# One compression gather's row copies placed behind the FFN, its loads a step ahead, and cached keys first in the sample attention's values

## The chip, the cores and the metric

The kernel runs on one core of one Trainium2 chip. The metric is device time in microseconds (us) of one launch that does the whole step; three runs of the kernel before the change gave 2105.78, 2105.80 and 2107.84, median 2105.8. The core has a matrix engine (PE, TensorE), VectorE (DVE), ScalarE (ACT), GpSimd (POOL) and a queue engine (SP) that issues most DMAs. Each engine works through its own instructions strictly in order and waits on semaphores of the others, so an instruction that waits also holds what is queued behind it on its engine.

## The reference

The model is two layers of a decoder over 576 tokens: 512 of a prompt and 8 each of 8 sample requests with 256 cached tokens. Layer 0 (even) mixes by a convolution and stick-breaking attention, layer 1 (odd) by sparse attention with compressed, selected and window branches. After each mixer come cross attention to a memory and a SwiGLU FFN. All is float32. What the change touches:

```python
def stick_breaking(q, k, v, q_pos, k_pos):     # k, v: cached rows, then the new ones
...
    w = jnp.where(mask, jnp.exp(jax.nn.log_sigmoid(z) + log_after), 0.0)
    return jnp.einsum('bhqk,bkhd->bqhd', w.astype(v.dtype), v)

def compress_blocks(kv, pe, w1, w2):           # odd layer, for k and for v
...
    blk = kv.reshape(B, nb, CMP_BLK, G, d) + pe[None, None, :, None, :]
    hid = jax.nn.gelu(jnp.einsum('bnlgd,ldh->bngh', blk, w1))
    return jnp.einsum('bngh,he->bnge', hid, w2)

def swiglu(a, w_gate, w_up, w_down):
    return (jax.nn.silu(a @ w_gate) * (a @ w_up)) @ w_down
```

The values of the attention are a sum over keys, so the order in which cached and new keys are added is free. The cached rows that the compression reads don't depend on anything computed, so they may be read at any time.

## The kernel before, in words

Activations lie feature by token in SBUF. Each large product takes float32 operands split in a high and a low part and is done as three products (high by high L308, low activation L309, low weight L310) summed in PSUM. Weights are loaded by SP into `raw` (three buffers), split by ACT (`wh`, L259) and DVE or POOL (`wl`, L261, L263) into two buffers each. Accumulators `acc` and transposes `wk` have four PSUM buffers each.

In the FFN, `fast.block` computes gate and up columns (L1172 to L1174, with `ga` and `gb` in PSUM; ACT keeps a sum in `gu`, L1255). DVE multiplies (`sg`, L1361), ACT and DVE make the halves `fH` and `fL` (L1366, L1367). `dense` then multiplies the down weights with these; after each accumulator DVE scales it (L1335) and adds it to the residual `h` (L341), which frees the accumulator.

The FFN of layer 0 goes in three chunks of columns. In the last (`c0 == 16`), a `tick` within the down product pumps a generator, `cmp_gather("k", 0, ...)`: the first quarter of the odd layer's compression, for which it reads the cached rows page by page. A gather has four steps; in each, four DMAs on SP (L1310, 64 KB each, 32 partitions) fill the first half of a buffer `cn` from the pool `knp` (three buffers, shared with others), DVE copies it regrouped into the second half (L1311), PE transposes it (L1316), and ACT and DVE evacuate it into `bt`. Three more gathers (second half of k, both of v) run in the odd layer's input product.

A scheduler lays down each engine's order from the order of the source, with priorities and the waits that it foresees; the generators only say where in the source a piece stands. So the first gather's copies stood on DVE between the last products of the FFN's block.

In the sample attention (two groups of four requests), the weights of the cached keys are transposed and evacuated into `wo` (two tiles, 128x512), those of the new tokens into `wn` (64x512); then `values` sums weights by values for four requests into `so` (L783): new tokens (`sbs`) first, then the cached keys from tiles that `take` loads (`sv`). In the trace these tiles read `vx` as they share a buffer of that name.

Of the kernel before, what the change touches and what calls it, by code (L numbers as in the profile page):

```python
# [94 lines left out]
def hybrid_step(ctx: ExitStack, tc: tile.TileContext, off, a, o):  # L95
    nc = tc.nc
# [17 lines left out]
    def KN(name):  # L114
        return knp.tile([128, 1024], FT, tag="kn", name=name)
# [41 lines left out]
    ident = cp.tile([128, 128], FT, name="ident")  # L157
# [528 lines left out]
    def sample_sb(sa, X, qT, kT, Vn, OHL):  # L686
# [10 lines left out]
        wn = X[:64, 1280:1792]  # L697
# [12 lines left out]
        for g in range(2):  # L710
# [7 lines left out]
            for b4 in range(4):  # L718
# [5 lines left out]
                for n2 in range(2):  # L724
                    p = WK()
# [33 lines left out]
            for b4 in range(4):  # L759
                x = en[:, b4][:, ::-1]  # L760
                nc.vector.tensor_tensor_scan(x, x, x, initial=1.0, op0=OP.mult, op1=OP.bypass)
                x = eo[:, b4][:, ::-1]
# [5 lines left out]
            wo = OHL[2], X[:, 0:512]  # L768
# [16 lines left out]
                                     skip_group_check=True, **kw)  # L785

            for b4 in range(4):
                values(b4, wn, Vn, start=b4 == 0, stop=False)
            for b4 in range(4):
                V = take()  # L790
                for n2 in range(2):
                    values(b4, wo[n2], V[:, n2 * 512:n2 * 512 + 512], start=False, stop=n2 == 1 and b4 == 3)
                yield 1
            os_ = X[:, 512:1024]
            evac(os_, O)
            yield 1
# [504 lines left out]
    cmp_w = 161  # L1301
    early_rows = {}

    def cmp_gather(x, h16, bt):
        for q4 in range(4):
            kn = KN("cn")
            for i in range(4):
                src = a["cache_nsa_cmp_" + x][0, ds(pages[q4 * 4 + i], 1)] \
                    .rearrange("a (n c l) g d -> (a n) c (l g d)", n=2, l=2)
                nc.sync.dma_start(kn[i * 32:i * 32 + 32, 0:512], src[:, h16 * 16:h16 * 16 + 16])  # L1310
            nc.vector.tensor_copy(kn[:, 512:1024].rearrange("p (g l d) -> p g l d", g=4, l=2),  # L1311
                                  kn[:, 0:512].rearrange("p (l g d) -> p g l d", l=2, g=4))
            yield 1
            p = WK()
            for g in range(4):
                nc.tensor.transpose(p[:, g * 128:g * 128 + 128], kn[:, 512 + g * 128:640 + g * 128], ident)  # L1316
            pv = p.rearrange("p (g b c) -> p g b c", g=4, c=16)
            for g in range(4):
                evac(bt[:, :, q4 * 32:q4 * 32 + 32].rearrange("p c (b g) -> p g b c", g=4)[:, g], pv[:, g])
            yield 1  # L1320


    def cmp_tile():
        return xtp.tile([128, 16 * cmp_w], FT, tag="bt", name="bt").rearrange("p (c n) -> p c n", n=cmp_w)
# [1 line left out]
    def ffn(l, fast, nxt):  # L1326
        wd = a["w_ffn_down"][l]
        kept = []

        def add_f(m, s0, n, p):  # L1330
            for c0, r in rs.items():
                x0, x1 = max(s0, c0), min(s0 + n, c0 + FH)
                if x1 > x0:
                    x = p[:, x0 - s0:x1 - s0]
                    nc.vector.tensor_mul(x, x, r[:, x0 - c0:x1 - c0])  # L1335
            add_h(m, s0, n, p)

        def into(b):
            if not kept:
                kept.extend(BIG(x, FR)[:, 0:4096].rearrange("p (b k m) -> p b k m", b=2, k=8) for x in ("dH", "dL"))  # L1340
            return [x[:, b] for x in kept]

        for c0, nch in ((0, 8), (8, 8), (16, 6)):
            HH, HL = v8(BIG("fH", FR)), v8(BIG("fL", FR))

            def down():
                ready.append(wblock(wd, c0, nch, 0, 256))
                yield 1

            for b0 in range(0, nch, 2):  # L1350
                sg = {}

                def out_gate(m, s0, p, own=False, sg=sg):
                    t = p if own else TMP("sg")[:, :FH]
                    ev_r(t, p, s0)
                    sg[m, s0] = t
                    return lambda: nc.scalar.activation(t, t, AF.Silu)

                def out_up(m, s0, p, own=False, sg=sg, b0=b0):
                    t = sg[m, s0]  # L1360
                    (nc.gpsimd if own else nc.vector).tensor_mul(t, p, t)  # L1361
                    e = nc.vector if b0 + 2 == nch and s0 == (1 - m) * FH else nc.gpsimd

                    def rest():
                        x = HH[:, b0 + m, s0:s0 + FH]
                        nc.scalar.activation(x, t, AF.Copy)  # L1366
                        e.tensor_sub(HL[:, b0 + m, s0:s0 + FH], t, x)  # L1367

                    return rest

                fast.block(out_gate, [])
                if b0 + 2 == nch:
                    later, fast.blocks = fast.blocks, []
                    fast.block(out_up, [down()])
                    fast.blocks = later
                    if not ready:
                        pump([down()], 1)
                else:
                    fast.block(out_up, [])
            if c0 < 16 or l == 0:  # L1380
                n_, rows0 = [0], []
                if c0 == 16:
                    early_rows["k"] = cmp_tile()
                    rows0 = [cmp_gather("k", 0, early_rows["k"])]

                def tick():
                    n_[0] += 1
                    if n_[0] % 5 == 4:
                        pump(rows0, 1)
                    if c0 < 16 and n_[0] == 50:  # L1390
                        fast.take()
                    if c0 < 16 and n_[0] in (54, 56, 58, 60):
                        pump(fast.G[1], 1)

                dense(wd, (HH, HL), c0, nch, 0, 1024, add_f, nxt=nxt if c0 == 16 else None, tick=tick,
                      parts=HV if c0 == 16 else ((0, FH), (FH, FH)))
        if l == 0:
            return
        out = [final(*HV[0])]
        W = [ready.pop(), wblock(wd, c0, nch, 256, 256)]  # L1400
        for s0, n in HV:
            s, late = slice(s0, s0 + n), None
            for m in range(8):
                WH, WL = W[m // 2]
                if s0 == 0 and m in (0, 2):
                    W.append(wblock(wd, c0, nch, m * 128 + 512, 256, into=into(m // 2)))
                ms = slice(m % 2 * 128, m % 2 * 128 + 128)
                p = ACC()[:, :n]
                for k in range(nch):
                    nc.tensor.matmul(p, WH[:, k, ms], HH[:, k, s], start=k == 0, stop=False)  # L1410
                    nc.tensor.matmul(p, WH[:, k, ms], HL[:, k, s], start=False, stop=False)  # L1411
                    nc.tensor.matmul(p, WL[:, k, ms], HH[:, k, s], start=False, stop=k == nch - 1)  # L1412
                    if s0 and k % 2:
                        pump(out, 1)
                if late is not None:
                    add_f(*late)
                late = m, s0, n, p
            add_f(*late)
            if s0 == 0:
                shift_states()  # L1420
        pump(out, 99)
        pump([final(*HV[1])], 99)
# [745 lines left out]
```

## Time and profile before

| | |
|---|---|
| median of three runs | 2105.8 us |
| profiled execution, time | 2100.41 us |
| its span | 2098.5 us |
| mean granted clock of PE | 0.981 |
| PE busy | 1977.1 us, 94% |
| PE weight loads | 86% |
| DVE busy | 1395.6 us, 67% |
| ACT, POOL busy | 46%, 40% |

The times of engines are of the one profiled execution; rows give microseconds from its span's start. PE is the engine that is nearly always busy, so the time is PE's work plus the gaps in it. [...] A row's bracket is the idle time of its engine just before it, with what ended it.

### The profile page before, as it was taken

Reading aid. Unit: us, or ns where it says so; the run is one execution under the profiler, and the core shown is the slowest. Engines: PE = TensorE matmul, PEld = TensorE weight load, DVE = VectorE, ACT = ScalarE, POOL = GpSimd, SP = SyncE. Lnnn points to the kernel's source line nnn. Section 1 sums busy time; section 2 is a strip of 40 time slices with the busy share of each in tenths; the row PEclk is TensorE's granted clock in tenths of the full one; section 3 lists DMA queues with packets and bytes.
Section 4 is the critical chain, followed back from the end, with each engine's and each line's share of the span. In section 5 each row is a group of like instructions: output and inputs, shape, how many; then the busy total and the mean of one; then the engine's idle time right before and its main releaser. Section 6 shows DMA issues by size and latency. Waiting matters only on the chain. (4 is left out here: it accounts for less than half of the span.)

```text
span 2098.5 us, 37416 instructions
## 1 busy us (share of the span) xinstructions
PE 1977.1 (94%) x14641; PEld 1811.3 (86%) x14641; DVE 1395.6 (67%) x2422; ACT 965.6 (46%) x2105; POOL 848.3 (40%) x774
## 2 busy tenths in 40 slices
PE   7999988999999999998899989999899989999998
PEld 6988855987889999998889967778887989999998
DVE  5469887544588577584646777765544787586675
ACT  5344555443455245153324537665444555254352
POOL 4355584422155235153313335563511355154252
PEclk9999998999999999999999999999999999999999
DMA  7445133255323222233344122212356222232323
GB/s 234 150 158 171 61 119 108 79 170 162 123 72 91 91 81 85 87 93 108 101 125 145 46 64 86 84 53 51 125 163 195 66 79 86 85 94 82 95 71 150
DMA packets 200797, 225.11 MB, mean 107 GB/s; under 512 B 13399, under 2 KB 179351, under 8 KB 200549
## 3 DMA queue, kind: packets, MB, share of 16 engines
q1 hardware_dynamic: 198317, 214.34, 32.7%
q0 software_dynamic: 2304, 8.39, 1.3%
q8 instruction: 115, 1.88, 0.4%
q14 instruction: 61, 0.50, 0.1%
HBM read 210.04 MB, written 17.08 MB: 108 GB/s over the span
## 5 line engine op out<-in xcount | busy, mean ns | idle before, releaser
L308 PE MATMUL acc<-aH,wh 128*128 128x256 f32 (+2 forms) x912 | 283.1, 310 | 2.5 <-DVE hpb L467 2.5
L263 POOL TENSOR_TENSOR wl<-raw,wh 128x1024 fp32r<-128x1024 f32 (+1 forms) x68 | 159.4, 2348 | 285.1 <-ACT wh L259 264.6
L310 PE MATMUL acc<-aH,wl 128*128 128x256 f32 (+2 forms) x912 | 272.6, 299 | 0.0
L309 PE MATMUL acc<-aL,wh 128*128 128x256 f32 (+2 forms) x912 | 271.7, 298 | 0.0
L259 ACT ACTIVATE wh<-raw 128x1024 fp32r<-128x1024 f32 (+1 forms) x174 | 167.3, 992 | 210.6 <-PE acc L309 77.2
L308 PE MATMUL acc<-fH,wh 128*128 128x288 f32 (+2 forms) x608 | 180.7, 297 | 3.1 <-DVE h L341 3.1
L309 PE MATMUL acc<-fL,wh 128*128 128x288 f32 (+2 forms) x608 | 180.6, 297 | 3.1 <-DVE fL L1367 3.1
L310 PE MATMUL acc<-fH,wl 128*128 128x288 f32 (+2 forms) x608 | 180.3, 297 | 0.2 <-POOL wl L263 0.2
L308 PEld LDWEIGHTS acc<-aH,wh 128*128 128x128 f32 (+1 forms) x912 | 173.7, 190 | 7.4 <-issue 3.3
L309 PEld LDWEIGHTS acc<-aL,wh 128*128 128x128 f32 (+1 forms) x912 | 173.6, 190 | 3.0 <-issue 2.5
L310 PEld LDWEIGHTS acc<-aH,wl 128*128 128x128 f32 (+1 forms) x912 | 173.0, 190 | 3.2 <-issue 2.9
L261 DVE TENSOR_TENSOR wl<-raw,wh 128x1024 fp32r<-128x1024 f32 (+1 forms) x106 | 144.2, 1373 | 31.3 <-ACT wh L259 27.6
L1139 POOL TENSOR_TENSOR wl<-raw,wl 128x512 fp32r<-128x512 f32 x44 | 69.0, 1569 | 187.2 <-ACT wl L1138 142.9
L1958 POOL TENSOR_TENSOR nar<-nar,f 128x512 f32<-128x512 f32 (+3 forms) x128 | 93.8, 755 | 88.0 <-DVE f L1956 60.6
L309 PEld LDWEIGHTS acc<-fL,wh 128*128 128x128 f32 x608 | 115.1, 189 | 4.2 <-DVE fL L1367 4.2
L308 PEld LDWEIGHTS acc<-fH,wh 128*128 128x128 f32 x608 | 115.0, 189 | 3.6 <-DVE h L341 3.3
L310 PEld LDWEIGHTS acc<-fH,wl 128*128 128x128 f32 x608 | 115.1, 189 | 0.4 <-POOL wl L263 0.4
L1367 POOL TENSOR_TENSOR fL<-sg,fH 128x288 fp32r<-128x288 f32 x76 | 77.7, 1023 | 59.0 <-ACT fH L1366 59.0
L341 DVE TENSOR_TENSOR h<-acc,h 128x288 f32<-128x288 f32 (+2 forms) x176 | 79.5, 454 | 32.1 <-PE acc L310 29.3
L1139 POOL TENSOR_TENSOR wh<-raw,wh 128x512 fp32r<-128x512 f32 x44 | 71.6, 1627 | 62.8 <-ACT wh L1138 62.6
L1335 DVE TENSOR_TENSOR acc<-acc,rs 128x288 f32<-128x288 f32 (+2 forms) x112 | 47.2, 422 | 72.1 <-PE acc L310 66.0
L1172 PE MATMUL gb<-x,wl 128*128 128x288 f32 x264 | 80.3, 304 | 14.1 <-ACT gu L1255 12.2
(540 smaller groups left out, 6402.7 us busy)
## 6 DMA issues: line engine op xcount, KB each, us to landing
raw<-in_w_ffn_gate_dram SPq DMA_DIRECT2D x44, 512.0 KB
raw<-in_w_ffn_up_dram SPq DMA_DIRECT2D x44, 512.0 KB
raw<-in_w_ffn_down_dram SPq DMA_DIRECT2D x40, 512.0 KB
ck<-in_cache_mem_k_dram SPq DMA_DIRECT2D x32, 512.0 KB
cv<-in_cache_mem_v_dram SPq DMA_DIRECT2D x32, 512.0 KB
raw<-in_w_in_even_dram SPq DMA_DIRECT2D x20, 512.0 KB
raw<-in_w_mem_k_dram SPq DMA_DIRECT2D x16, 512.0 KB
raw<-in_w_mem_v_dram SPq DMA_DIRECT2D x16, 512.0 KB
```

Of the source, the lines that this page charges most:

```text
L259: last[1] = nc.scalar.activation(hi, x, AF.Copy)
L261: nc.vector.tensor_sub(lo, x, hi)
L263: nc.gpsimd.tensor_sub(lo, x, hi)
L308: nc.tensor.matmul(po, WH[:, k, ms], H[:, k, s], start=k == 0, stop=False)
L309: nc.tensor.matmul(po, WH[:, k, ms], L[:, k, s], start=False, stop=False)
L310: nc.tensor.matmul(po, WL[:, k, ms], H[:, k, s], start=False, stop=k == nk - 1)
L341: nc.vector.tensor_add(h[:, m, s0:s0 + n], p, h[:, m, s0:s0 + n])
L1139: eng.tensor_sub(L, x, H)
L1172: nc.tensor.matmul(po, WH[:, k], H[:, k], start=start and k == 0, stop=False, skip_group_check=True)
L1335: nc.vector.tensor_mul(x, x, r[:, x0 - c0:x1 - c0])
L1367: e.tensor_sub(HL[:, b0 + m, s0:s0 + FH], t, x)
L1958: nc.gpsimd.tensor_tensor(P[:, x, :n], P[:, x, :n], f[:, x:x + 1].to_broadcast([128, n]), op=OP.mult)
```

## The change

In `values`' callers the cached keys come first and the new tokens last. `cmp_gather` has a new first step that only loads, and loads the next step's rows before it copies the present ones; so it has nine steps instead of eight. For the first gather the copies are tied, in order and not by a semaphore, behind the last DVE instruction that had been issued when the down product of the last chunk begins, and the tick that pumps it comes every fourth time instead of every fifth.

```diff
--- before.py
+++ after.py
@@ -785,12 +785,12 @@
                                      skip_group_check=True, **kw)
 
             for b4 in range(4):
-                values(b4, wn, Vn, start=b4 == 0, stop=False)
-            for b4 in range(4):
                 V = take()
                 for n2 in range(2):
-                    values(b4, wo[n2], V[:, n2 * 512:n2 * 512 + 512], start=False, stop=n2 == 1 and b4 == 3)
-                yield 1
+                    values(b4, wo[n2], V[:, n2 * 512:n2 * 512 + 512], start=b4 == n2 == 0, stop=False)
+                yield 1
+            for b4 in range(4):
+                values(b4, wn, Vn, start=False, stop=b4 == 3)
             os_ = X[:, 512:1024]
             evac(os_, O)
             yield 1
@@ -1301,24 +1301,35 @@
     cmp_w = 161
     early_rows = {}
 
-    def cmp_gather(x, h16, bt):
-        for q4 in range(4):
-            kn = KN("cn")
+    def cmp_gather(x, h16, bt, behind=None):
+        kn = {}
+
+        def load(q4):
+            t = kn[q4] = KN("cn")
             for i in range(4):
                 src = a["cache_nsa_cmp_" + x][0, ds(pages[q4 * 4 + i], 1)] \
                     .rearrange("a (n c l) g d -> (a n) c (l g d)", n=2, l=2)
-                nc.sync.dma_start(kn[i * 32:i * 32 + 32, 0:512], src[:, h16 * 16:h16 * 16 + 16])
-            nc.vector.tensor_copy(kn[:, 512:1024].rearrange("p (g l d) -> p g l d", g=4, l=2),
-                                  kn[:, 0:512].rearrange("p (l g d) -> p g l d", l=2, g=4))
+                nc.sync.dma_start(t[i * 32:i * 32 + 32, 0:512], src[:, h16 * 16:h16 * 16 + 16])
+
+        load(0)
+        yield 1
+        for q4 in range(4):
+            if q4 < 3:
+                load(q4 + 1)
+            t = kn.pop(q4)
+            c = nc.vector.tensor_copy(t[:, 512:1024].rearrange("p (g l d) -> p g l d", g=4, l=2),
+                                      t[:, 0:512].rearrange("p (l g d) -> p g l d", l=2, g=4))
+            if behind is not None:
+                tc.add_manual_dep(c.ins, behind, mybir.DependencyInfo(
+                    mybir.DependencyClass.NoSync, mybir.DependencyReason.DATA), reason="program order")
             yield 1
             p = WK()
             for g in range(4):
-                nc.tensor.transpose(p[:, g * 128:g * 128 + 128], kn[:, 512 + g * 128:640 + g * 128], ident)
+                nc.tensor.transpose(p[:, g * 128:g * 128 + 128], t[:, 512 + g * 128:640 + g * 128], ident)
             pv = p.rearrange("p (g b c) -> p g b c", g=4, c=16)
             for g in range(4):
                 evac(bt[:, :, q4 * 32:q4 * 32 + 32].rearrange("p c (b g) -> p g b c", g=4)[:, g], pv[:, g])
             yield 1
-
 
     def cmp_tile():
         return xtp.tile([128, 16 * cmp_w], FT, tag="bt", name="bt").rearrange("p (c n) -> p c n", n=cmp_w)
@@ -1381,11 +1392,12 @@
                 n_, rows0 = [0], []
                 if c0 == 16:
                     early_rows["k"] = cmp_tile()
-                    rows0 = [cmp_gather("k", 0, early_rows["k"])]
+                    rows0 = [cmp_gather("k", 0, early_rows["k"], next(
+                        i.name for i in reversed(nc.cur_bb.bb.instructions) if str(i.engine).endswith("DVE")))]
 
                 def tick():
                     n_[0] += 1
-                    if n_[0] % 5 == 4:
+                    if n_[0] % 4 == 3:
                         pump(rows0, 1)
                     if c0 < 16 and n_[0] == 50:
                         fast.take()
```

The number of instructions of each engine is the same. Lines below the change move down by 9 to 12 (the copy L1311 is L1320 after, the product L1361 is L1372).

DVE at the end of the last FFN block of layer 0, before (`sg`, `gu`, `fL` belong to the block; `cn` are the gathered rows, `wl` the low halves of down weights):

```order
L1311 COPY cn_10173<-cn_10173 128x512
L242 TENSOR_TENSOR sg_10015<-gb_9848,rs_6409 128x288
L1311 COPY cn_10268<-cn_10268 128x512
L1215 TENSOR_TENSOR acc_9887<-acc_9887,gu_6441 128x288
L242 TENSOR_TENSOR sg_10056<-acc_9887,rs_6415 128x288
L261 TENSOR_TENSOR wl_10031<-raw_10036,wh_10030 128x512
L1311 COPY cn_10356<-cn_10356 128x512
L1361 TENSOR_TENSOR sg_9959<-ga_9980,sg_9959 128x288
L1257 TENSOR_TENSOR sg_10098<-acc_10017,gu_6441 128x288
L1361 TENSOR_TENSOR sg_10015<-gb_9981,sg_10015 128x288
L261 TENSOR_TENSOR wl_10138<-raw_10139,wh_10137 128x1024
L1367 TENSOR_TENSOR fL_9350<-sg_10015,fH_9349 128x288
```

The same stretch after, from the last but one of these rows on (those above it are the same without the three copies):

```order
L261 TENSOR_TENSOR wl_10138<-raw_10139,wh_10137 128x1024
L1378 TENSOR_TENSOR fL_9350<-sg_10015,fH_9349 128x288
L1215 TENSOR_TENSOR acc_10017<-acc_10017,gu_6441 128x288
L1372 TENSOR_TENSOR sg_10056<-acc_10017,sg_10056 128x288
L1526 COPY bt_10136<-vt_93 128x16
L1346 TENSOR_TENSOR acc_10147<-acc_10147,rs_6409 128x256
L1378 TENSOR_TENSOR fL_9350<-sg_10056,fH_9349 128x288
L341 TENSOR_TENSOR h_92<-acc_10147,h_92 128x256
L1320 COPY cn_10166<-cn_10166 128x512
L1320 COPY cn_10199<-cn_10199 128x512
L1320 COPY cn_10282<-cn_10282 128x512
L214 SCALAR_TENSOR_TENSOR aL_10584<-h_92,vt_93,aH_10583 128x256
```

The three copies of cached rows have moved from between the block's products to behind the first sum into `h`.

DVE at the end of the layer's down product, before (`acc` scaled and `h` summed for one output tile after the other, `var` the norm's statistic):

```order
L341 TENSOR_TENSOR h_92<-acc_10514,h_92 128x256
L214 SCALAR_TENSOR_TENSOR aL_10584<-h_92,vt_93,aH_10583 128x256
L1335 TENSOR_TENSOR acc_10535<-acc_10535,rs_6409 128x32
L1335 TENSOR_TENSOR acc_10535<-acc_10535,rs_6415 128x288
L341 TENSOR_TENSOR h_92<-acc_10535,h_92 128x320
L214 SCALAR_TENSOR_TENSOR aL_10584<-h_92,vt_93,aH_10583 128x320
L1335 TENSOR_TENSOR acc_10556<-acc_10556,rs_6409 128x32
L1311 COPY cn_10863<-cn_10863 128x512
L1335 TENSOR_TENSOR acc_10556<-acc_10556,rs_6415 128x288
L261 TENSOR_TENSOR wl_10674<-raw_10675,wh_10673 128x1024
L341 TENSOR_TENSOR h_92<-acc_10556,h_92 128x320
L261 TENSOR_TENSOR wl_10674<-raw_10679,wh_10673 128x1024
```

And after, from the sum of accumulator `acc_10492` on:

```order
L341 TENSOR_TENSOR h_92<-acc_10492,h_92 128x256
L1320 COPY cn_10811<-cn_10811 128x512
L1346 TENSOR_TENSOR acc_10514<-acc_10514,rs_6409 128x256
L214 SCALAR_TENSOR_TENSOR aL_10584<-h_92,vt_93,aH_10583 128x256
L341 TENSOR_TENSOR h_92<-acc_10514,h_92 128x256
L214 SCALAR_TENSOR_TENSOR aL_10584<-h_92,vt_93,aH_10583 128x256
L1346 TENSOR_TENSOR acc_10535<-acc_10535,rs_6409 128x32
L1346 TENSOR_TENSOR acc_10535<-acc_10535,rs_6415 128x288
L341 TENSOR_TENSOR h_92<-acc_10535,h_92 128x320
L214 SCALAR_TENSOR_TENSOR aL_10584<-h_92,vt_93,aH_10583 128x320
L1346 TENSOR_TENSOR acc_10556<-acc_10556,rs_6409 128x32
L1346 TENSOR_TENSOR acc_10556<-acc_10556,rs_6415 128x288
```

The copy that stood between the two scalings of the last tile now stands ahead of three sums into `h`.

PE where the values of the second group begin, before (`sbs` new tokens, `sv` cached keys, `L308` to `L310` the output projection):

```order
L194 MATMUL rsb<-ident,var 128x128 x2
L194 MATMUL rsb<-ident,var 128x64
L783 MATMUL so<-sbs,vx 32x128 x16
L783 MATMUL so<-sv,vx 32x128 x6
L308 MATMUL acc<-oH,wh 128x256
L783 MATMUL so<-sv,vx 32x128 x2
L568 MATMUL wk<-ident,sba 128x128 x2
L783 MATMUL so<-sv,vx 32x128
L309 MATMUL acc<-oL,wh 128x256
L310 MATMUL acc<-oH,wl 128x256
```

And after:

```order
L194 MATMUL rsb<-ident,var 128x128 x2
L194 MATMUL rsb<-ident,var 128x64
L783 MATMUL so<-sv,vx 32x128 x8
L568 MATMUL wk<-ident,sba 128x128
L783 MATMUL so<-sv,vx 32x128 x16
L568 MATMUL wk<-ident,sba 128x128
L783 MATMUL so<-sv,vx 32x128
L568 MATMUL wk<-ident,sba 128x128 x2
L308 MATMUL acc<-oH,wh 128x256
L568 MATMUL wk<-ident,sba 128x128
```

The products on cached keys come first, with transposes of the convolution between them; the 16 on new tokens follow far behind, among the output projection's.

## Rows read from the trace of the kernel before

**Rows 1.** Waits of PE, 930 to 1150 us: who for whom, total, times, longest.

```profile
PE gb L1172 <- ACT gu L1255: 9.7, 1, 9.7
PE hid L1537 <- DMA w<-in_cmp_w_k_dram: 4.6, 3, 2.7
PE rsb L194 <- POOL var L188: 3.7, 1, 3.7
...
PE acc L308 <- DVE h L341: 3.1, 1, 3.1
```

**Rows 2.** Timeline of DVE, 948 to 974 us: start, duration, operation, idle before it.

```profile
953.98 0.75 DVE L1311 COPY cn<-cn 128x512 f32<-128x512 f32 x1 [5.03 <-DMA cn<-in_cache_nsa_cmp_k_dram]
...
961.02 0.43 DVE L1311 COPY cn<-cn 128x512 f32<-128x512 f32 x1 [5.94 <-DMA cn<-in_cache_nsa_cmp_k_dram]
...
962.24 0.68 DVE L261 TENSOR_TENSOR wl<-raw,wh 128x512 fp32r<-128x512 f32 x1
966.68 0.43 DVE L1311 COPY cn<-cn 128x512 f32<-128x512 f32 x1 [3.76 <-DMA cn<-in_cache_nsa_cmp_k_dram]
967.02 0.45 DVE L1361 TENSOR_TENSOR sg<-ga,sg 128x288 f32<-128x288 f32 x1
```

**Rows 3.** Timeline of ACT, 960 to 978 us.

```profile
967.86 0.39 ACT L1255 ACTIVATE gu<-gb 128x288 f32<-128x288 f32 x1
968.15 0.62 ACT L259 ACTIVATE wh<-raw 128x512 fp32r<-128x512 f32 x1
```

**Rows 4.** Timeline of PE, 954 to 976 us.

```profile
968.30 0.61 PE L1172 MATMUL gb<-x,wl 128*128 128x288 f32 x1 [9.67 <-ACT gu L1255]
...
971.29 0.30 PE L1172 MATMUL acc<-x,s4w 128*128 128x288 f32 x1
...
974.33 0.39 PE L309 MATMUL acc<-fL,wh 128*128 128x256 f32 x1
```

**Rows 5.** Timeline of SP's queue, 944 to 975 us.

```profile
945.81 10.08 SPq L1310 DMA_DIRECT2D cn<-in_cache_nsa_cmp_k_dram  x12
962.94 11.36 SPq L271 DMA_DIRECT2D raw<-in_w_ffn_down_dram  x4
```

**Rows 6.** Windows: length, busy by engine (PE, PEld, DVE, ACT, POOL), clock, DMA share, GB/s.

```profile
947.00:955.00 8.00, 8.00 (x61) 7.86 (x60) 2.93 (x5) 2.45 (x5) 2.60 (x3) 1.00 0.12 43
...
1012.00:1019.00 7.00, 5.79 (x22) 5.80 (x23) 6.17 (x14) 2.84 (x8) 2.71 (x3) 0.51 0.56 161
...
1029.00:1034.00 5.00, 5.00 (x27) 5.00 (x27) 1.47 (x5) 1.19 (x3) 0.00 (x0) 0.66 0.31 89
330.00:350.00 20.00, 15.09 (x108) 9.19 (x104) 15.94 (x23) 11.54 (x23) 8.80 (x8) 0.76 0.23 66
```

**Rows 7.** Timeline of DVE, 1004 to 1014 us.

```profile
1009.61 1.41 DVE L1311 COPY cn<-cn 128x512 f32<-128x512 f32 x1 [3.02 <-DMA cn<-in_cache_nsa_cmp_k_dram]
...
1011.53 1.22 DVE L261 TENSOR_TENSOR wl<-raw,wh 128x1024 fp32r<-128x1024 f32 x1
1012.67 0.48 DVE L341 TENSOR_TENSOR h<-acc,h 128x320 f32<-128x320 f32 x1
```

**Rows 8.** Timeline of PE, 1092.5 to 1105 us.

```profile
1093.72 1.36 PE L1537 MATMUL hid<-kvA,w 128*128 128x161 f32 x8 [1.15 <-DMA w<-in_cmp_w_k_dram]
...
1101.07 2.52 PE L1537 MATMUL hid<-kvA,w 128*128 128x161 f32 x8 [2.70 <-DMA w<-in_cmp_w_k_dram]
```

**Rows 9.** Timeline of DVE, 1019 to 1030 us.

```profile
1023.24 0.43 DVE L1311 COPY cn<-cn 128x512 f32<-128x512 f32 x1 [2.84 <-DMA cn<-in_cache_nsa_cmp_k_dram]
...
1027.08 0.15 DVE L187 TENSOR_SCALAR var<-ssp 128x2 f32<-128x2 f32 x1
```

**Rows 10.** Timeline of PE, 336 to 347 us.

```profile
343.83 1.93 PE L783 MATMUL so<-sbs,vx 64*32 64x128 f32 x32 [4.91 <-DVE vx L141]
```

**Rows 11.** Timeline of DVE, 333 to 346 us.

```profile
339.56 0.66 DVE L141 COPY vx<-wk 128x512 f32<-128x512 f32 x1
...
343.10 0.68 DVE L141 COPY vx<-wk 64x512 f32<-64x512 f32 x1
```

## The prediction

> **What bounds the kernel now.** I read the page's busy shares first: PE works 94% of the span, so a gain must come out of PE's idle time or out of stretches at the lower clock, and only two places change. Then PE's waits around the row copies [rows 1]: the list is headed by one wait of 9.7 us of `gb` L1172, and `rsb` 3.7 and `acc` 3.1 belong to the same stage; the reader is to see that each is a single wait. The `hid` waits (4.6 in 3) are for weights loaded through POOL, which the change leaves where they were. The chain behind the 9.7 us follows from DVE's and ACT's timelines. DVE reached its three row copies before their data: it sat 5.03, 5.94 and 3.76 us in front of them [rows 2]. Only behind the third could it do the product `sg` at 967.02, then ACT evacuated `gu` at 967.86 [rows 3], then PE went on at 968.30 [rows 4]. The copies feed nothing that PE needs there; they stand in front of what it needs. The loads can't be faster: 12 loads of 64 KB issued in 10.1 us [rows 5], with a DMA share of 0.12, which is 2 of 16 engines, at 43 GB/s [rows 6]; 256 KB per copy at that pace is 6.1 us, and the copies' ends lie 7.0 and 5.7 us apart [rows 2].
>
> For the other edit the same view of the sample attention shows PE waiting 4.91 us for an evacuation of `vx` before it starts the values [rows 10], and DVE reaching that evacuation (64x512, the new tokens' weights) only at 343.10, when its own copy for the cached keys (128x512) had ended at 340.2 [rows 11].
>
> **Edit 1, the copies behind the FFN's blocks.** No instruction is added or removed on any engine; the first three copies stand behind the blocks' last product and the first `h` sum, and the fourth's load is one step ahead.
>
> The 9.67 us and the slow clock behind it go. The 12 products after it start every 0.24 us, from 968.30 to 971.29 are 2.99 us [rows 4], twice what they take at full speed, so 1.4 us more: 11.1 us is the most that is there. What is late next is the weights of the down projection. Their load is at 962.94 on SP, behind the row loads [rows 5], and waits for DVE's `wl` at 962.24 [rows 2]; with the copies gone DVE reaches that some 6 us earlier, so the load is issued near 957. But the row loads keep their place on SP and their two engines until the third copy's data is there, 966.68 [rows 2]. The weight load of 256 KB goes over all 16 engines, as far as the DMA shares show, so its sixteenths on those two stand behind: about 32 KB at 43 GB/s is 0.7 us, 967.4. ACT's copy `wh` of these weights (0.62 us [rows 3]) stands ahead of the other `fH` copies (0.44 us), so the last product group of the first down block can start near 968.6, where it was 974.33 [rows 4]. Without that wait PE would be there at 963.1: the 958.63 at which it stopped, 1.5 us for the 12 products at full speed, and the 3.0 us from 971.29 to 974.33. So a new wait of 5.5 us stands in place of 9.67, gain 974.3 - 968.6 = 5.7, less 1.4 for a clock that falls again: **4.2 us**. Bounds: 11.1 if the weights land early; 0 if they land no earlier than before. Less than nothing I exclude here, since no load is issued later.
>
> The trace has the two engines' worth in the share of 0.12 [rows 6] and the weights used at 968.15, 1.5 us after the last row copy's data although issued 5.2 us before [rows 2, 3, 5]. [...]
>
> Then the copy at 1009.61. [...] In the new order the load is no sooner against PE (the three buffers bind it), so most of the wait stays, but the sum stands ahead of `wl`, which gives 1.2 back. Whether the clock falls for a shorter idle decides the rest: it stayed at full speed after 1.15 us (8 products in 1.36) and fell after 2.70 (2.52) [rows 8]; 1.8 us lies between, so I take half of 2.8. 1.2 + 1.4 = **2.6 us**, bounds 0 and 5.9.
>
> The copy at 1023.24 held the statistic `var` back until 1027.08 (2.84 us of wait, then two `wl` and the last sums) [rows 9], and PE waited 3.7 for its broadcast `rsb` [rows 1], then ran at 0.66 for 5 us [rows 6], 1.7 lost: 5.4 in all. Now its load follows at once on the one before and the copy stands nine places earlier on DVE. `var` still stands behind two `wl` of 1.2. I take 3.7 - 0.7 = 3.0 of idle and 0.5 of the clock: **3.5 us**. If the rows land late, the copy now holds the last three `h` sums instead; a wait as long as before, 2.84, would then cost PE what the earlier copy did, so the bounds are 5.4 and -0.5.
>
> The rest of the gathers (second half, values) lands a step earlier as well, but PE waited there for weights and arithmetic [rows 1]: 0, bounds 1.5 to either side, from the 2.7 us `hid` wait, of which the loads share the engines.
>
> **Edit 2, cached keys first.** PE may start its values as soon as the cached keys' weights are evacuated, of which DVE's is the last and ends at 340.2, not at 343.8 [rows 11]: up to 3.6 us. But PE then reaches the output projection earlier, and this needs the low halves `oL` of the normalised convolution, which DVE makes behind that same evacuation, so not before 344. So PE waits there again. What is gained is the work that moves into the hole: some 24 of the 32 products on cached keys and a few transposes. The 16 on new tokens (32 passes in the trace) took 1.93 us at the lower clock [rows 10]; 24 of 32 at the upper one are 24 x 0.12 / 2 = 1.5: **1.5 us**. Bounds: +6 (hole and part of a clock of 0.76 over 20 us [rows 6] that holds 4.8 us of loss), and -3, since the scheduler also reorders DVE and ACT in the 40 us before, and one more wait as long as those of 3 us [rows 1] may come of it.
>
> **Sum.** 4.2 + 2.6 + 3.5 + 0 + 1.5 = 11.8 us from the profiled execution's 2100.41 (span 2098.5). That execution lies 5.4 below the median 2105.8, 0.26%; the same 11.8 from the median gives **2094.0 us**. The bounds added: 29.9 to -5.0.
>
> **Rivals.** (a) All of it: the weights land early, the clock falls nowhere. For it: [rows 4] show the whole 11.1 behind copies alone. Against it: the row loads' place on the queue. 11.1 + 4 + 5 + 4 = 24 us, 2082. (b) The waits move: the weights' share lands behind 968, and 2.6 and 3.5 shrink to half because the copies still wait for their rows at 43 GB/s. Left are about 2 + 1 + 1.5 + 0 = 4.5 us, 2101. For it: the loads get no engine more, and DVE waited 3.02 and 2.84 us for the later copies too [rows 7, 9]. Against it: the first three hold 14.7 us of waits [rows 2], and these leave the blocks. (c) Slower: the copy now nine places earlier meets its rows late. Its load is issued behind the one before, and the odd projection's weights of 512 KB stand behind both; if it lands more than some 4 us after DVE gets there, the `h` sums stand still, PE runs out of accumulators and begins the odd layer at half clock. It costs 4 + 2.8 there and about 4 more when the weights behind it come late too, 10.8; with nothing from the three smaller terms, -0.5 for the even layer's and 4.2 at the blocks the kernel is 7 us slower: 2113. It decides from where the loss there exceeds 4.2, a landing some 2 us behind DVE.
>
> **Chances.** Gain of 8 to 16 us: 0.50 (own range 2090 to 2098). (a) 0.16. (b) 0.22, about half of it inside what a measurement can tell apart, 0.2% or 4.2 us. (c) 0.12, a quarter of it within. So faster 0.77, same 0.14, slower 0.09. The range leaves out the ends of (a) and (c): 2083 to 2105.
>
> **What would show it.** Right: no wait of `gb` for `gu` near 958; the three copies in a row with no wait; a new PE wait of 4 to 6 us in the first down block, for ACT's `fH` behind `wh`, some clock lost behind it; `rsb`'s wait under 1.5; the values starting near 340.5 with a wait for `oL` behind them. Wrong: no wait in the first down block (then (a)), a copy that waits over 3 us ahead of `h` sums and PE idle beside it (then (c)), or an even layer that ends later than before.

## The result and the profile after

The changed kernel took 2094.25 us (median of three runs, 2093.45 to 2094.89), 0.9942 of the kernel before [0.9919, 0.9964]. Its profiled execution took 2094.25 us, its span is 2092.2, the mean granted clock 0.984 of full speed; against the profiled execution of before that is 6.3 us of span. A larger sample is below: twelve more runs of the same kernel gave 0.9978 [0.9965, 0.9991], which puts the gain at about 5 us, not at the 11.8 of the prediction's sum.

PE's waits from 925 to 1145 us in the changed kernel, to be held against [rows 1]:

```profile
PE hid L1549 <- DMA w<-in_cmp_w_k_dram: 5.9, 3, 3.4
PE acc L308 <- ACT fH L1377: 4.9, 1, 4.9
PE acc L308 <- DVE h L341: 3.8, 1, 3.8
PE rsb L194 <- POOL var L188: 2.1, 1, 2.1
...
PE gb L1172 <- ACT gu L1255: 0.6, 1, 0.6
```

The 9.7 us of `gb` for `gu` has gone, and one wait of 4.9 us for `fH` stands in its place. `rsb` fell from 3.7 to 2.1; the wait for the sum into `h` did not fall, it rose from 3.1 to 3.8.

The new wait in the first down block, on SP's queue, ACT and PE:

```profile
945.39 10.09 SPq L1312 DMA_DIRECT2D cn<-in_cache_nsa_cmp_k_dram  x12
955.58 15.28 SPq L271 DMA_DIRECT2D raw<-in_w_ffn_down_dram  x4
```
```profile
966.38 0.63 ACT L259 ACTIVATE wh<-raw 128x512 fp32r<-128x512 f32 x1 [8.29 <-DMA raw<-in_w_ffn_down_dram]
966.91 0.76 ACT L1377 ACTIVATE fH<-sg 128x288 fp32r<-128x288 f32 x2
```
```profile
967.73 0.58 PE L308 MATMUL acc<-fH,wh 128*128 128x256 f32 x1 [4.93 <-ACT fH L1377]
968.58 0.58 PE L309 MATMUL acc<-fL,wh 128*128 128x256 f32 x1 [0.28 <-DVE fL L1378]
968.96 0.41 PE L310 MATMUL acc<-fH,wl 128*128 128x256 f32 x1
...
972.38 0.33 PE L308 MATMUL acc<-fH,wh 128*128 128x256 f32 x1
```

The weight load is issued 7.4 us earlier than in [rows 5], yet its data lets ACT go on only at 966.38, which is when the third copy's rows came in the kernel before (966.68 in [rows 2]). ACT stood 8.29 us in front of `wh`, with the two `fH` queued behind it. The 16 products from 968.96 to 972.38 take 3.42 us, where products of this shape start every 0.12 us at a clock of 1.00 (1015.00 to 1016.92); at the 0.50 of this stretch 1.5 us of the gain is given back there.

The three copies themselves have nothing to wait for, but the later one has, and it is slow (DVE, then POOL beside it, then PE):

```profile
970.65 1.08 DVE L1320 COPY cn<-cn 128x512 f32<-128x512 f32 x3
...
1006.20 2.48 DVE L1320 COPY cn<-cn 128x512 f32<-128x512 f32 x1 [2.46 <-DMA cn<-in_cache_nsa_cmp_k_dram]
...
1009.47 0.49 DVE L341 TENSOR_TENSOR h<-acc,h 128x320 f32<-128x320 f32 x1
...
1012.53 0.41 DVE L1320 COPY cn<-cn 128x512 f32<-128x512 f32 x1
...
1018.44 1.22 DVE L261 TENSOR_TENSOR wl<-raw,wh 128x1024 fp32r<-128x1024 f32 x1
...
1020.04 1.21 DVE L261 TENSOR_TENSOR wl<-raw,wh 128x1024 fp32r<-128x1024 f32 x1
1021.17 0.15 DVE L187 TENSOR_SCALAR var<-ssp 128x2 f32<-128x2 f32 x1
```
```profile
1006.06 2.34 POOL L263 TENSOR_TENSOR wl<-raw,wh 128x1024 fp32r<-128x1024 f32 x1 [2.09 <-ACT wh L259]
```
```profile
1010.01 0.64 PE L308 MATMUL acc<-fH,wh 128*128 128x320 f32 x1 [3.79 <-DVE h L341]
...
1014.29 0.28 PE L308 MATMUL acc<-aH,wh 128*128 128x256 f32 x1
```

Copies of this shape took 0.41 to 0.43 us where POOL was idle (1012.53 here, [rows 9]). This one began 0.14 us after POOL's `wl` and ended 0.28 us after it (1008.68 against 1008.40), 2.48 us. The one of [rows 7] took 1.41, and POOL's row in the kernel before shows why: its `wl` ended at 1010.74, the copy at 1011.02, again 0.28 us later.

```profile
1008.34 2.40 POOL L263 TENSOR_TENSOR wl<-raw,wh 128x1024 fp32r<-128x1024 f32 x1 [1.01 <-ACT wh L259]
```

**The time by stretches.** Whole times of one kernel scatter by 10 us, so the experiments are also read by the start of the same sums into `h` (DVE, L341) in every trace (one execution each). The stretch "blocks" goes from the sum at 881.18 us in before to the one at 976.04, "rest" from there to 1459.67; in the changed kernel:

```profile
880.78 0.45 DVE L341 TENSOR_TENSOR h<-acc,h 128x288 f32<-128x288 f32 x1
...
970.31 0.41 DVE L341 TENSOR_TENSOR h<-acc,h 128x256 f32<-128x256 f32 x1
...
1454.06 0.49 DVE L341 TENSOR_TENSOR h<-acc,h 128x320 f32<-128x320 f32 x1 [0.26 <-PE acc L310]
```

| kernel | ratio to before | blocks | rest | both |
|---|---|---|---|---|
| before | 1 | 94.9 | 483.6 | 578.5 |
| changed | 0.9942 [0.9919, 0.9964] | 89.5 | 483.8 | 573.3 |
| e1 changed, again | 0.9978 [0.9965, 0.9991] | 89.6 | 482.5 | 572.1 |
| e2 keys first only | 0.9999 [0.9986, 1.0012] | 94.3 | 484.9 | 579.2 |
| e3 gathers only | 0.9978 [0.9965, 0.9991] | 89.7 | 485.2 | 574.9 |
| e10 tie only | 0.9943 [0.9922, 0.9965] | 89.8 | 480.2 | 570.0 |
| e11 loads ahead only | 1.0001 [0.9984, 1.0017] | 94.6 | 482.6 | 577.2 |
| e4 `fH` first on ACT | 0.9930 [0.9913, 0.9947] | 84.6 | 482.4 | 567.0 |
| e6 weights first on SP | 0.9949 [0.9932, 0.9966] | 84.4 | 489.3 | 573.7 |
| e7 copies on ACT | 0.9967 [0.9952, 0.9982] | 89.7 | 483.9 | 573.6 |
| e5 16 partitions | 0.9858 [0.9837, 0.9879] | 83.6 | 468.1 | 551.8 |
| e8 16 and `fH` first | 0.9850 [0.983, 0.987] | 84.6 | 465.0 | 549.6 |
| e9 16, before's order | 0.9863 [0.9839, 0.9887] | 84.6 | 467.9 | 552.5 |
| e12 16, changed, again | 0.9870 [0.9847, 0.9893] | 84.6 | 467.2 | 551.8 |

The rest agrees within 2.7 us where edit 1 is the same (changed, e1, e3), the blocks within 0.2. e1 to e4 ran on one chip, e5 to e8 on a second and e9 to e12 on a third, each group beside the kernel before (medians 2102.78, 2105.31 and 2103.70), so times of different groups are set against each other only by their ratios. One of e8's six executions took 4945.96 us; its ratio, and its median of 2075.54 below, leave it out.

### The profile page after: what moved, and what is told of

It reads as the page before. It is cut to its first block, busy times and chain, and to the rows that moved or that the text cites. A ratio compares the mean times of both kernels' runs of the same rounds, so it can differ in the third digit from the quotient of the medians.

```text
span 2092.2 us, 37416 instructions
## 1 busy us (share of the span) xinstructions
PE 1977.6 (95%) x14641; PEld 1812.4 (87%) x14641; DVE 1392.5 (67%) x2422; ACT 965.5 (46%) x2105; POOL 850.6 (41%) x774
## 5 line engine op out<-in xcount | busy, mean ns | idle before, releaser
L308 PE MATMUL acc<-aH,wh 128*128 128x256 f32 (+2 forms) x912 | 282.9, 310 | 2.5 <-DVE hpb L467 2.5
L310 PE MATMUL acc<-aH,wl 128*128 128x256 f32 (+2 forms) x912 | 272.8, 299 | 0.0
L308 PE MATMUL acc<-fH,wh 128*128 128x288 f32 (+2 forms) x608 | 181.5, 298 | 8.7 <-ACT fH L1377 4.9
L309 PE MATMUL acc<-fL,wh 128*128 128x288 f32 (+2 forms) x608 | 181.2, 298 | 3.5 <-DVE fL L1378 3.5
L310 PE MATMUL acc<-fH,wl 128*128 128x288 f32 (+2 forms) x608 | 180.7, 297 | 0.2 <-POOL wl L263 0.2
L308 PEld LDWEIGHTS acc<-aH,wh 128*128 128x128 f32 (+1 forms) x912 | 173.5, 190 | 7.4 <-issue 3.3
L310 PEld LDWEIGHTS acc<-aH,wl 128*128 128x128 f32 (+1 forms) x912 | 173.2, 190 | 3.1 <-issue 2.9
L308 PEld LDWEIGHTS acc<-fH,wh 128*128 128x128 f32 x608 | 115.8, 191 | 9.5 <-ACT fH L1377 5.4
L310 PEld LDWEIGHTS acc<-fH,wl 128*128 128x128 f32 x608 | 115.6, 190 | 0.4 <-POOL wl L263 0.4
L341 DVE TENSOR_TENSOR h<-acc,h 128x288 f32<-128x288 f32 (+2 forms) x176 | 79.5, 454 | 31.8 <-PE acc L310 28.9
L1172 PE MATMUL gb<-x,wh 128*128 128x288 f32 x264 | 80.7, 306 | 9.4 <-ACT gu L1255 6.9
```

The source lines that it names most:

```text
L308: nc.tensor.matmul(po, WH[:, k, ms], H[:, k, s], start=k == 0, stop=False)
L309: nc.tensor.matmul(po, WH[:, k, ms], L[:, k, s], start=False, stop=False)
L310: nc.tensor.matmul(po, WL[:, k, ms], H[:, k, s], start=False, stop=k == nk - 1)
L341: nc.vector.tensor_add(h[:, m, s0:s0 + n], p, h[:, m, s0:s0 + n])
L1172: nc.tensor.matmul(po, WH[:, k], H[:, k], start=start and k == 0, stop=False, skip_group_check=True)
```

## The experiments

**e1, the changed kernel once more**, and the two edits apart: **e2** has the order of `values` alone, **e3** the gathers alone (the hunks of the diff above, without the other).

> The changed kernel once more, in five rounds. The two profiled executions differ by 6.3 us in span (2098.5 to 2092.2), the medians of three runs by 11.55. Theory: the change is worth what the traces show, 6 to 7 us, ratio about 0.9968, and the rest is how the three runs of the kernel before fell (5.4 us above its own profiled execution). Rival: the change is worth 11 to 12 us, ratio about 0.9945, and the profiled execution of before was one that missed a wait.

> Only the second edit (cached keys first); gathers as before. Theory, from the offsets of the two traces around the sample attention (1.44 us late before it, 0.2 early behind it): 1.6 us faster, ratio 0.9992, with nothing changed behind 700 us. Rival: the scheduler's reordering eats it and the ratio is 1.000 or above; then all of the gain is the gathers'.

> Only the first edit (copies behind the blocks, loads a step ahead); values as before. Theory: 5.6 us faster than before (trace offset 0.4 at 881 us, 6.0 at 1143), ratio 0.9973, with a wait of 4 to 5.5 us of acc for fH in the first down block. Rival: the edits need each other, and alone it gives less than 3 us.

e1: 2097.0 us against 2102.78, twelve runs from 2092.57 to 2104.4, before from 2097.49 to 2108.65. A gain of 5.8 by the medians, 1.9 to 7.4 by the interval (times 2103): 11 to 12 is out on this chip. e2 could not be told from before in time, and PE's waits around the gathers stayed (the long one of `gb` 9.0, `rsb` 5.1). e3 gives what the whole gives. So edit 1 carries the change: 5.3 us at the blocks, and nothing measurable behind them.

**e10 and e11, the halves of edit 1.** e10 ties the copies but loads each step's rows in that step; e11 loads ahead with the copies where the scheduler puts them:

```diff
# e10, against the changed kernel
-        load(0)
-        yield 1
...
-            if q4 < 3:
-                load(q4 + 1)
+            load(q4)
# e11, against the changed kernel
-                    rows0 = [cmp_gather("k", 0, early_rows["k"], next(
-                        i.name for i in reversed(nc.cur_bb.bb.instructions) if str(i.engine).endswith("DVE")))]
+                    rows0 = [cmp_gather("k", 0, early_rows["k"])]
...
-                    if n_[0] % 4 == 3:
+                    if n_[0] % 5 == 4:
```

> The changed kernel without the loads a step ahead: the first gather's copies are tied behind the blocks, each step loads its own rows. Theory (the tie gives the blocks' 4 us, the early loads the 1.5 to 2 us at the even layer's end): gb's wait is gone, a wait for fH of 4 to 6 us stands in its place, rsb's wait is 3.5 or more, ratio 0.998 to 0.999. Rival (the early loads give all of it): ratio 0.9995 or more.

> The changed kernel without the tie: loads a step ahead, copies where the scheduler puts them. Theory: the 9 to 10 us wait of gb for gu stays, rsb's wait is 2 to 3.5, ratio 0.999 to 1.000. Rival (loads a step ahead let the copies find their rows): gb's wait under 6 us and a ratio of 0.997 or less.

The tie alone took 2091.35 us, the loads ahead alone 2104.37 on the same chip, where the kernel before took 2103.70: the tie gives the time, the loads ahead gave none. In the stretches e10 takes 570.0 against 572.1 to 574.9 with both; whether it is faster than the whole change isn't shown, as the two didn't run on one chip. PE's waits from 915 to 1145 us, of e10 and of e11:

```profile
PE acc L308 <- ACT fH L1374: 4.9, 1, 4.9
```
```profile
PE gb L1172 <- ACT gu L1255: 9.8, 2, 9.2
```

The wait for `fH` is as expected in e10, and the long one of `gb` stayed in e11. Three of my numbers missed: the ratio of e10, 0.9943 where I had 0.998 to 0.999, and `rsb`, which waits 2.6 in e10, without loads ahead, where I had 3.5 or more, and 4.2 in e11, where I had 2 to 3.5. So the tie, with the copies' places that follow from it, is enough to shorten that wait. With the loads ahead PE waits 5.9 and 1.6 us for the compression's weights `w` (k and v), in e10 3.8 and none; whether the earlier row loads cause that wasn't tried by itself.

**e4, the new wait taken away on ACT**: the two `wh` copies of the second down block stand behind the last `fH`. **e6, the same on SP**: the row loads stand behind that block's last weight load.

```diff
# e4, where ACT's wh is issued; hold_act holds, twice, the name of the last ACT instruction (fH)
+            if hold_act:
+                tc.add_manual_dep(last[1].ins, hold_act.pop(), mybir.DependencyInfo(
+                    mybir.DependencyClass.NoSync, mybir.DependencyReason.DATA), reason="program order")
# e6, in load(); weights holds the name of that block's last weight load
-                nc.sync.dma_start(t[i * 32:i * 32 + 32, 0:512], src[:, h16 * 16:h16 * 16 + 16])
+                d = nc.sync.dma_start(t[i * 32:i * 32 + 32, 0:512], src[:, h16 * 16:h16 * 16 + 16])
+                if behind is not None:
+                    tc.add_manual_dep(d.ins, weights, mybir.DependencyInfo(
+                        mybir.DependencyClass.NoSync, mybir.DependencyReason.DATA), reason="program order")
```

> The changed kernel, with ACT's two copies wh of the second down block's weights tied behind the four fH copies that PE needs for the first block. Theory: PE's new wait of 4.93 us near 963 comes from ACT's order alone (the wh copy waits 8.29 us for weights that stand behind the gathered rows on two DMA engines, and fH stands behind it), so it goes, with the half clock behind it: 4.9 + 2.0, some 5 to 7 us faster than the changed kernel. Rival: the second block's weights are then late, and PE waits the same time some 10 us on: no gain.

> The changed kernel with the first gather's row loads placed behind the last load of the second down block's weights on SP. Theory: these weights land by 960, and the wait for fH goes; the rows start 10 us later (SP waits until 955 for the weights' buffer), the third lands near 973, and DVE's copies wait up to 5 us ahead of sums into h; PE has four accumulators, so half of it is felt. 2 to 5 us faster than the changed kernel. Rival: ACT's wh waits as before for another reason, no gain, and the later rows cost 3 to 6 us.

In both the wait for `fH` is gone and the blocks end 5.0 to 5.2 us sooner. ACT's `wh` of these weights, in e4 and in e6:

```profile
965.91 0.63 ACT L259 ACTIVATE wh<-raw 128x512 fp32r<-128x512 f32 x1 [2.88 <-DMA raw<-in_w_ffn_down_dram]
```
```profile
960.29 0.63 ACT L259 ACTIVATE wh<-raw 128x512 fp32r<-128x512 f32 x1 [0.40 <-DMA raw<-in_w_ffn_down_dram]
```

In e4 the weights are as late as in the changed kernel, and PE doesn't feel it: its wait came from ACT's order. In e6, with the rows behind the load, they are there 8.5 us sooner, counted from the start of the stretch (879.74 in e4, 882.59 in e6): the load is late because the rows stand before it. e4 keeps the gain (2089.11 us against 2097.0 of e1 on the same chip); e6 pays it back by the stretches, its rest is 489.3, with 6.5 us of waits for `h` in four (longest 2.5). Its rows start later and DVE waits 20.6 us in 6 for those of k, where it waits 12.7 in 4 in the changed kernel.

**e5, the rows over more engines**, and with it e8 (e5 and e4 together), e12 (e5 again) and **e9 (these loads in the kernel before, no other change)**:

```diff
-                nc.sync.dma_start(t[i * 32:i * 32 + 32, 0:512], src[:, h16 * 16:h16 * 16 + 16])
+                for n in range(2):
+                    nc.sync.dma_start(t[i * 32 + n * 16:i * 32 + n * 16 + 16, 0:512], src[n, h16 * 16:h16 * 16 + 16])
```

> The changed kernel with each page's row load cut into two loads of 16 partitions (32 KB each, so eight a step). Theory: a load of 32 partitions in two parts runs on two DMA engines, and the down weights' share waits behind it there; loads of 16 partitions go over 16, so the weights, issued near 957, land by 961, the wait of acc for fH falls from 4.9 us to under 1.5 and the kernel is 4 to 7 us faster than the changed one, if the eight issues (0.8 us each on SP, 6.6 a step) don't make later copies later. Rival: the weights wait for something else (their issue, memory), the wait stays at 4 to 5.

> The fH order of the fourth run together with the loads of 16 partitions. Theory: both remove the same wait, so this is no faster than the fH order alone by more than what the later copies give (acc for h 3.8 us, rsb 2.1): 0 to 4 us. Rival: they add, 5 us or more over the fH order.

> The kernel before in its own order, with each page's rows loaded by two DMAs of 16 partitions. Theory (the rows' two engines were the loss, the order of the copies only moves where it is paid): the copies find their rows, the 9.7 us wait of gb for gu falls under 2.5, and most of the gain over the kernel before is there without the change: ratio 0.986 to 0.990, the change on top worth under 4 us. Rival (the order matters as much): each copy still waits for a load issued in its own step, some 2.3 us to landing, gb's wait stays at 3 to 5 us, rsb's at 3 or more, and the ratio is 0.991 to 0.995.

> The changed kernel with rows loaded by DMAs of 16 partitions once more, beside the kernel before with the same loads. Theory: 0.984 to 0.988 of the kernel before, and up to 4 us under the kernel before with the same loads. Rival: more than 6 us under it.

e5 took 2077.66 us, some five times the gain of the change and far more than I expected. e9 took 2076.63 and e12 2077.13 on one chip: with these loads the reordering is worth nothing that can be measured, and the rival of e9 fell, but for `rsb`. `gb` waits 0.6 in e9; only `rsb` waits longer than in e12 (4.3 and 2.5), as the rival had it. e8, 2075.54, is 2 us under e5, within the scatter: the wait that e4 took away isn't there any more. But it lies 17.4 us under e4 in the stretches, where I had 0 to 4, so the finer loads do more than remove that wait.

The windows from 946 to 980 us of the changed kernel and of e9 (columns as in [rows 6]):

```profile
946.00:980.00 34.00, 28.79 (x200) 28.04 (x199) 15.84 (x34) 11.83 (x26) 11.42 (x10) 0.90 0.38 123
```
```profile
946.00:980.00 34.00, 33.40 (x253) 32.94 (x252) 23.11 (x44) 16.85 (x36) 16.31 (x14) 1.00 0.42 125
```

In e9 PE works nearly all the time, at a clock of 1.00. How the loads differ is in the DMA view of 947 to 955 us, where rows are all that moves, of before and of e5 (first the share of the 16 engines, in tenths, in slices of 0.2 us):

```profile
DMA  0230000111111111111111111111111111111111
...
DMA packets 178, 0.34 MB, mean 43 GB/s; under 512 B 10, under 2 KB 10, under 8 KB 178
```
```profile
DMA  0000000313216023070240210211304033031230
...
DMA packets 416, 0.43 MB, mean 53 GB/s; under 512 B 208, under 2 KB 208, under 8 KB 416
...
cn<-in_cache_nsa_cmp_k_dram SPq DMA_DIRECT2D x14, 32.0 KB, 1.7
```

0.34 MB are some 5 loads of 64 KB, 0.43 MB are 13 of 32 KB. The small packets are 10 / 5 = 2 for each load before and 208 / 13 = 16 now. I read them as one for each engine that carried a part; the 2 fit the share of 0.12, 1.9 of 16 engines, and of the 16 the share shows some 11, as slices of e5 reach 0.7 where before stays at 0.1 from the eighth on. The rate rose little, from 43 to 53 GB/s; what changed, as I read it, is that no engine has a long line of rows in front of a weight load. DVE's waits for rows from 940 to 1145 us come to 47.6 us in 13 before, 41.5 in 12 after and 1.8 in 3 in e9. SP's order differs too: weight loads stand between the rows in e5 and e9. e6 shows that order alone can give the blocks their 5 us, but not the rest its 15 (483.6 to 467.9 in e9): in e6 it is longer. How much of the 15 the order of the finer loads adds wasn't tried, so that the number of engines alone gives the 27 us of e9 isn't shown.

**e7, the copies on ACT** (`nc.scalar.activation(..., AF.Copy)` for `nc.vector.tensor_copy`, tied behind ACT's last instruction instead of DVE's):

> The changed kernel with all sixteen regrouping copies on ACT in place of DVE. In the traces a DVE copy of 0.43 us took 1.28 to 2.48 us wherever POOL's wl (2.4 us, 128x1024) ran beside it, and ended 0.27 to 0.28 us behind POOL. Theory: it is held by POOL, ACT isn't: no copy takes over 1 us on ACT, and PE's wait of acc for h near 1006 falls from 3.8 to about 1.7. Rival: whatever reads and writes 128x512 beside POOL is slow; ACT's copies take 1.3 to 2.5 us there too, and the wait stays. The time may go either way, since ACT's own queue is held while it waits for rows.

A copy that ran beside POOL's `wl` (992.79, 2.42 us long), and the one at the place in question, where POOL's now comes later:

```profile
993.14 0.62 ACT L1320 ACTIVATE cn<-cn 128x512 f32<-128x512 f32 x1
1005.98 0.63 ACT L1320 ACTIVATE cn<-cn 128x512 f32<-128x512 f32 x1 [3.25 <-DMA cn<-in_cache_nsa_cmp_k_dram]
```

None of ACT's copies was held, and PE's wait for `h` fell from 3.8 to 2.7 (1.7 was expected). In the stretches it bought nothing (573.6 against 573.3): `rsb` waited 3.5 and the transposes 4.2 (2.1 and 1.9 in the changed kernel). ACT now stands still for the rows in DVE's place, 40.2 us in 11; that this is the cause of the two longer waits is my reading and wasn't tried.

## Why the prediction was right and wrong

The time, 2094.0 against 2094.25, was met by luck, by two errors that cancel: the sum was 11.8 and the change gives about 6 (5.2 in the blocks and the rest, and perhaps 1 in the sample attention), while the median of the three runs before lay 3 us above that of the first larger sample (2102.78) and that after 3 us below its own (2097.0). That these are draws of one scatter is my reading: the changed kernel was run again on one chip alone, and its variants e6, e7 and e10 came out 7 to 12 us faster than the kernel before on two others, with stretches only 4.8 to 8.5 us shorter. By size the outcome is nearest rival (b), 4.5 us, and its reason, the copies that still wait for their rows, is half of what happened. The working itself has small slips: 5.7 - 1.4 is 4.3 and 24 x 0.12 / 2 is 1.4, which cancel in the sum; the copies' starts lie 7.0 us apart, their ends 6.7; and a clock of 0.76 costs 3.6 us of the 15.09 that PE is busy [rows 6], not 4.8, in the bound of edit 2.

- **Blocks, 4.2:** right in mechanism and size. The `fH` wait was to be 5.5 us and was 4.93, the product group was to start at 968.6 and started at 968.58, in a trace that is 0.4 us ahead at the stretch's start; 5.3 us less in the stretch, 1.5 given back to the clock, nearly all behind the stretch's end: 3.8. That the weights' share stands behind the rows on two engines was my estimate, from the 0.12 [rows 6] and the 1.5 us between the last copy's start and the weights' use [rows 2, 3]; no run shows the engines' own order. e6 shows that its cause is the weight load behind the rows, e4 that it reaches PE by ACT's order.
- **The copy at 1009.61, 2.6:** this step failed. PE lost 5.9 before: 3.05 of wait [rows 1], which less 1.2 is the 1.8 of the prediction, and, as I work it out, 2.8 of the 5.79 us that it was busy at a clock of 0.51 [rows 6], of which the 1.4 is half; after, 3.79 idle, and 18 products in 4.28 us (1010.01 to 1014.29) where 18 x 0.15 = 2.7 would do (the last six go at that pace): 5.4 in all, so 0.5 gained (0.7 more of idle, 1.2 less of clock). The sum did come ahead of `wl` as I had it and DVE's wait for rows fell to 2.46. But the copy was taken as of one length in either order; it had grown from 1.41 to 2.48 as it now meets POOL's `wl` from its start, and two scalings and an evacuation stand between it and the sum.
- **`rsb`, 3.5:** mis-sized. 1.6 of idle and 0.1 of the clock were gained. `var` moved only as far as the two `wl` of 1.2 let it, from 1018.44 to 1021.17; I had named them and then taken 3.0 of 3.7. The forecast "under 1.5" was 2.08.
- **Later gathers, 0:** PE's waits there went from 7.7 us (4.6 for `w` of k, 3.1 of the transposes behind `nar`) to 9.4 (5.9 for `w` of k, 1.6 for that of v, 1.9), a little over the bound of 1.5; in e1, the same program, they come to 7.8 (5.3, 1.5, 1.0), so no loss is shown.
- **Keys first, 1.5:** the size can't be refuted, the path was wrong. (The lower clock of the 1.93 us was 0.50, from 343.83 to 345.76 us in before.) The values did not start near 340.5 but at 346.02, and PE waited ahead of them for something not named:

```profile
342.10 1.97 PE L772 MATMUL wk<-ident,sbs 128*128 128x128 f32 x8 [2.90 <-POOL sbs L764]
...
346.02 1.08 PE L783 MATMUL so<-sv,vx 128*32 128x128 f32 x16
```
```profile
343.94 0.66 DVE L141 COPY vx<-wk 128x512 f32<-128x512 f32 x1
```
```profile
339.22 2.83 POOL L764 TENSOR_TENSOR sbs<-sbs,vx 128x1020 f32<-128x1020 f32 x1 [0.62 <-DVE vx L763]
```

  In the kernel before POOL's same operation stood here:

```profile
334.55 2.00 POOL L764 TENSOR_TENSOR sbs<-sbs,vx 128x1020 f32<-128x1020 f32 x1
```

  The cached keys' weights are made on POOL (`sbs`), transposed by PE and only then evacuated. In the new order POOL's operation starts 4.7 us later, behind a scan of DVE (L763) that ends at 339.14 instead of 334.47; so the transposes come at 342.10 and DVE's evacuation ends at 344.6 instead of 340.2. The prediction had reckoned with the old order of DVE and POOL, and the wait for `oL` that it named didn't come. From DVE's operation on `hpb` at 190.25 us (L467) to the sum at 371.95 the eleven traces with this edit take 181.2 us on average (179.9 to 182.1), the three without 182.4 (181.7, 181.9, 183.5). 1.2 us, less than the scatter, and nothing in e2's time.
- **"The loads can't be faster"** was the dearest sentence. It was true of the loads as written, and it was written beside the share of 0.12, 2 of 16 engines, that should have turned the question round. The order of the copies was worth some 6 us, the form of the loads, with the order on SP that came of it, 27 (e9).

## What to carry to other kernels

Where a queue's transfers run at a small, constant DMA share, as the 0.12 here, first try another cut of the transfer (27 us in e9), and only then the order of who waits for it (some 6). An edit that takes a wait off one engine can move it to whatever is queued behind the same late data; name that queue and price it, as the 4.9 us here. Compare stretches between the same instructions in two traces when whole times scatter by more than the effect.

## What the runs showed of the hardware

- DVE copies of 128x512 from SBUF to SBUF that began while POOL's `wl` ran ended after it in these five cases: they took 2.48 and 1.99 (changed), 1.28 and 1.41 (before) and 2.51 us (e10), and each ended 0.27 to 0.28 us after POOL's operation; where POOL was idle a copy took 0.43 [rows 9]. One that began first wasn't held: in e6 it took 0.43, and POOL's operation, 0.01 us behind it, 2.65 where those above took 2.34 to 2.42 (other work of DVE ran beside it too, so its length isn't put down to the copy alone):

```profile
1007.21 0.43 DVE L1324 COPY cn<-cn 128x512 f32<-128x512 f32 x1 [2.31 <-DMA cn<-in_cache_nsa_cmp_k_dram]
```
```profile
1007.22 2.65 POOL L263 TENSOR_TENSOR wl<-raw,wh 128x1024 fp32r<-128x1024 f32 x1 [2.10 <-ACT wh L259]
```

  ACT's copy that ran beside POOL's `wl` in e7 took 0.62 us, the one without it 0.63. Why DVE's were held isn't shown.
- Unchanged code differed by up to 8.8 us between executions. From one sum into `h` to the next across the second layer's cross attention (1487.86 to 1625.04 in the changed kernel) the 14 traces take either 136.3 to 139.7 us (eight) or 142.8 to 145.1 (six), whatever the kernel; changed and e1, one program, took 137.2 and 144.9. PE's waits there, 1490 to 1660 us, of the changed kernel and of e1:

```profile
PE wk L881 <- DMA ck<-in_cache_mem_k_dram: 5.3, 7, 2.4
```
```profile
PE wk L881 <- DMA ck<-in_cache_mem_k_dram: 8.7, 6, 2.5
```

  The granted clock fell with them: 0.89 from 1490 to 1520 us in e1, 1.00 in the other. Why these loads come late in some executions stays open.
